# 512 more columns of the down product as seven products of 256, one up group less, and two weight sums made in DRAM

## The chip, the core and the metric

The kernel runs on one core of a Trainium2 chip. The metric is device time in microseconds (us) of one execution, the median over several runs. PE is TensorE, PEld its weight loads, DVE is VectorE, ACT is ScalarE, POOL is GpSimd, and SP is SyncE, whose queue sends out nearly all DMAs.

## What is computed

One encoder block over 272 positions (16 meta tokens and 256 others), width 2048, in float32: a normalisation, two kinds of attention side by side, an output projection with residual, and then a gated MLP with residual. The change lies in the MLP, which in the reference is

```python
def conv_glu(x, w_gate, w_up, conv_w, conv_b, w_down):
    L = x.shape[1]
    g = x @ w_gate
    u = x @ w_up
    pad = CONV_W // 2
    gp = jnp.pad(g, ((0, 0), (pad, pad), (0, 0)))
    gc = conv_b
    for i in range(CONV_W):
        gc = gc + conv_w[i] * gp[:, i:i + L]
    return (jax.nn.silu(gc) * u) @ w_down
...
    h = h + conv_glu(rmsnorm(h, ffn_norm_g[l]), w_gate[l], w_up[l], conv_w[l], conv_b[l], w_down[l])
return h[:, N_META:]
```

`w_gate` and `w_up` are 2048 x 5632, `w_down` is 5632 x 2048, and the 256 positions that are not meta tokens are returned.

## The kernel before

**Precision.** A float32 product is made of single-pass products: each operand is split into a high part (rounded, ScalarE) and a low part (the rest, VectorE), and high x high, high x low and low x high are summed in PSUM. Weights are therefore loaded in pieces of up to 1024 columns of 128 rows (512 KB; `raw`), split by ScalarE into `whi` (L239, called by `split_hi`) and by VectorE into `wlo` (L243, `split_lo`), and used by PE. There are four `whi` and four `wlo` buffers, so the splits run at most four pieces ahead of PE, and six `raw` buffers in the MLP.

**Plain tiles.** Gate tiles (128 of the 5632 columns) take three matmuls of 258 columns for each 128 rows of weights (L607 to L609). Plain up and down tiles take two (`mm2`, L1875 and L1876): the high weights against the high and low activations side by side, 512 columns, then the low weights against the high activations, 256. The last down tile takes three of 256. I call each such set of matmuls for one 128 x 128 weight tile a block. A piece of 1024 is eight blocks.

**Seven products.** Where a 2 x 2 block product would need eight products, a scheme makes it of seven, from sums of blocks on both sides. Here a pair of contraction tiles (256 rows) against Q columns is cut into 2 x 2 blocks: the weights' quarters are Q/2 wide, the activations' quarters are 128 positions. Four sums of weight quarters are made by VectorE (`weight_sums`), four sums of activation quarters in `value_sums`; those are kept as split parts in DRAM (`s_up`, `s_down`) or in the unfilled end of the activation buffer (`near`), and loaded back into two buffers (`sin`). A pair is a `RowPair`, its pieces are `Quarters`, and `scheme_products` issues 7 x 3 matmuls (L279). The kernel before uses it in two places:

- *Up groups* (`QUADS`): six groups of four up tiles (512 columns), each 8 pairs; products of 256 columns. The two pieces of a pair hold 768 and 1024 columns: the three quarters used as they are, and the four sums. The sums take VectorE one operation of 512 and two of 256 for each pair.
- *The wide group*: 1024 of the 2048 down columns (`SF`), 22 pairs; products of 512 columns. A pair has pieces of 1024, 512, 1024 and 1024 columns, and its sums take one operation of 1024 and two of 512.

Weights' quarters lie in the order A, B, C, D = upper left, upper right, lower right, lower left; the sums are C or B less A or B, and further differences of these.

**Order.** A list `work` holds all MLP pieces in PE's order. First come gate and up tiles, plain, up to the first group. Then a stretch for each group: its 16 pieces are spread evenly among the gate and up pieces of the stretch (six tiles for the first four groups, eight for the last two). Then the down product: three plain pieces (`AHEAD`), the 88 pieces of the wide group among plain down pieces, and eight plain pieces at the end (`BEHIND`). A plain down tile has 44 blocks: five pieces of 1024 and one of 512. The instruction order of every engine is written out by a planner in the kernel (`Flow`), from its own costs; on the chip each engine runs its list in that order and waits by semaphores. One list `pieces` orders the loads, too (`load_weights`, L489 on SP's queue).

**Buffers.** When the last up tile has been used, the memory of the split activations of the MLP's input becomes two buffers of 2048 columns for the wide group's weights (`quarters`) and two for their sums (`sums4`). Of the eight PSUM banks, an up group holds four until its output is taken, the wide group seven.

**Outputs.** Plain down tiles come out transposed (`down_out`): for all but the last one, ScalarE copies and three POOL additions and products scale them and add the residual, then a DMA writes them. The wide group's output (`scheme_out`) is combined by VectorE from the seven banks, scaled by ScalarE, added to the residual by POOL and written by four DMAs. `EARLY` pairs of the MLP input's activation sums go to DRAM before the attention's buffers are free; the residual of the wide columns is transposed beforehand.

Of the kernel before, what the change touches and what calls it, by code (L numbers as in the profile page):

```python
# [45 lines left out]
SF = 1024  # L46
ST = SF // P
QUADS = (4,10,16,22,28,36)


def near_to(g):

    return sum(f <= FC - KC + 2 * g for f in (*QUADS, FC)[1:])

# [3 lines left out]
AHEAD, BEHIND = 3, 8  # L58
PAIR_PRIO = 3
# [147 lines left out]
def encoder_block(ctx: ExitStack, tc: tile.TileContext, io):  # L207
# [138 lines left out]
    class Quarters(Piece):  # L346
# [3 lines left out]
        def __init__(self, pair, products, *segments):  # L350
            self.pair, self.products, self.segments = pair, products, segments
            self.slices([n for _, _, n in segments])
            self.n = sum(n for _, _, n in segments)
            self.there = [
                pair.loaded if kind == "raw" else pair.summed[a + n > 2 * pair.q]
                for kind, a, n in segments
            ]

        def release(self):
            self.pair.used(self.segments[0][0])  # L360

        def views(self, i):
            kind, a, n = self.segments[i]
            t = self.parts[i]
            src = self.pair.raw if kind == "raw" else self.pair.sums
            return src[:, a : a + n], self.hi[:, t], self.lo and self.lo[:, t]

    class RowPair:


        def __init__(self, src, g, q):
            self.src, self.g, self.q = src, g, q
            self.loaded, self.summed, self.ev_S = Event(), [Event(), Event()], Event()
            if q == PW // 2:
                self.pieces = [
                    Quarters(self, (3, 2), ("raw", 2 * q, 2 * q)),
                    Quarters(self, (1,), ("raw", 0, q)),
                    Quarters(self, (5, 7), ("sums", 0, 2 * q)),
                    Quarters(self, (6, 4), ("sums", 2 * q, 2 * q)),
                ]  # L380
                self.slots = {"raw": quarters, "sums": sums4}
            else:
# [4 lines left out]
                self.slots = {"raw": raws, "sums": raws}  # L387
            n = len(self.pieces) // 2
            self.left = {"raw": n + 1, "sums": n}

        def used(self, kind):
            self.left[kind] -= 1
            if self.left[kind] == 0:
                fl.put(self.slots[kind], getattr(self, kind))

    quarters, sums4, s_parts = Slots([]), Slots([]), Slots([])
# [45 lines left out]
    for w, f in enumerate(QUADS):  # L442

        g, end = f // 2, (*QUADS, FC)[w + 1] // 2
# [4 lines left out]
        for i in range(KC // 2):  # L449
            r = RowPair(io["w_up_s"][w][i], i, PW // 4)  # L450
            r.first, r.last, r.of, r.quad = i == 0, i == KC // 2 - 1, "up", f
# [3 lines left out]
        lead, tail = 3, 4 if w == len(QUADS) - 1 else 2  # L455
# [12 lines left out]
    scheme = []  # L468
    for g in range(FC // 2):
        r = RowPair(io["w_down_s"][g], g, PW // 2)  # L470
        r.first, r.last, r.of, r.near = g == 0, g == FC // 2 - 1, "down", False
        scheme += [(p, "scheme", r, 0) for p in r.pieces]
    n = len(others) - BEHIND
    work += others[:AHEAD]
    for i in range(AHEAD, n):
        k = 4 if others[i - 1][2] != others[i][2] else 2
        work += scheme[:k] + [others[i]]
        del scheme[:k]
    work += scheme + others[n:]
# [25 lines left out]
    def load_pair(r):  # L505
        if r.of == "up":
            r.raw, r.sums = yield raws, 2
        else:
            r.raw = yield from one(quarters)
        def load_S():  # L510
            if r.near:
                r.ev_S = ev_near[r.g]
                return
            r.S = yield from one(s_parts)
            src, saved = saved_sums[r.of][r.g]
# [4 lines left out]
        if r.of == "up":  # L520
            yield from load_S()
        for a in range(0, 4 * r.q, PW):
            yield "sp", 600
            ev = r.loaded if a + PW == 4 * r.q else Event()
            load(r.raw[:, a : a + PW], r.src[:, a : a + PW], ev, nc.sync)
        if r.of == "down":
            yield from load_S()
        fl.spawn(weight_sums(r), (lambda: 0) if r.of == "up" else 2)

    def weight_sums(r):  # L530
        yield r.loaded
        if r.of == "down":
# [1682 lines left out]
```

## Time and profile before

| | us |
|---|---|
| median of three runs (1109.08 to 1109.53) | 1109.18 |
| the profiled execution | 1109.0 |
| its span, from its first to its last instruction | 1107.1 |

The granted TensorE clock is 1.0 throughout. The page's slices show DMA and its rate over the span, 27.7 us each:

```profile
DMA  9553434443654696656645667677588697777862
GB/s 327 194 172 124 147 128 151 139 162 134 230 189 159 205 338 212 216 188 207 255 167 184 236 209 277 211 272 244 181 300 298 225 331 254 250 263 263 280 251 76
```

The first row is the mean busy share of the 16 DMA engines in tenths (9 is 90% or more), the second what they moved. The attention lies in slices 1 to about 11, the output projection behind it, the MLP from about 400 us (slice 15) on, and the wide down group from about 870 us to 1083 us. Rows of a window are: the window, its length, then for each engine busy time and number of instructions, the granted clock, the DMA share and GB/s. A timeline row has start, duration, engine, line, operation, what it writes and reads, the count, and in brackets the engine's idle time before it. A duration may reach into the next instruction's start, so that the time that one instruction adds is read from start to start.

### The profile page before, as it was taken

To read this page: it belongs to the slowest core of one execution; us is meant where nothing else is said; L and a number is where in the kernel's file an instruction comes from. 1 tells how busy PE (TensorE), PEld (TensorE's weight loads), DVE (VectorE), ACT (ScalarE), POOL (GpSimd) and SP (SyncE) were. 2 spreads that over 40 slices of the span, in tenths; PEclk is the share of its full clock that TensorE was granted. 3 is DMA by queue.
4 is the path that set the end of the run, shared out by engine and by line. 5 is a ranking of instruction groups with operands and counts; after the bars stand their busy time and mean duration, and the time that the engine had idled before them with its cause. 6 is when DMAs were issued, how large, how long until landed. Compare 5 with 4: busy or idle time off the path is not lost.

```text
span 1107.1 us, 21940 instructions
## 1 busy us (share of the span) xinstructions
PE 1099.9 (99%) x8094; PEld 1046.2 (95%) x8094; DVE 1000.8 (90%) x1857; ACT 740.7 (67%) x1490; POOL 140.9 (13%) x202
## 2 busy tenths in 40 slices
PE   9999999999999999999999999999999999999998
PEld 9999999999999999999999999999999888888888
DVE  8979888888878989999999999988999999999984
ACT  8788979798647676656665665666556565655663
POOL 3211222121433400000000000000000011100114
PEclk9999999999999999999999999999999999999999
DMA  9553434443654696656645667677588697777862
GB/s 327 194 172 124 147 128 151 139 162 134 230 189 159 205 338 212 216 188 207 255 167 184 236 209 277 211 272 244 181 300 298 225 331 254 250 263 263 280 251 76
DMA packets 72372, 239.36 MB, mean 216 GB/s; under 512 B 8137, under 2 KB 12745, under 8 KB 72265
## 3 DMA queue, kind: packets, MB, share of 16 engines
q1 hardware_dynamic: 71976, 237.69, 61.8%
q8 instruction: 63, 1.03, 0.4%
q14 instruction: 45, 0.36, 0.1%
q10 hardware_dynamic: 288, 0.27, 0.1%
HBM read 219.44 MB, written 17.83 MB: 214 GB/s over the span
## 4 chain that ended last, share of the span: by engine, by line
PE 81%; DVE 9%; ACT 5%; DMA 3%; issue 2%; POOL 0%; DVEq 0%; SPq 0%; ACTq 0%; POOLq 0%
PE bank L279 21%; PE bank L607 13%; PE bank L609 13%; PE bank L608 13%; PE bank L1875 12%; PE bank L1876 6%; DVE wlo L243 4%; PE bank L285 2%; ACT whi L239 2%; DMA s_down<-sums 1%; ACT scr L239 1%; DVE mt L243 1%; DVE scr L251 1%; DMA s_up<-sums 1%; DVE raw L243 1%
## 5 line engine op out<-in xcount | busy, mean ns | idle before, releaser
L239 ACT ACTIVATE whi<-raw 128x512 fp32r<-128x512 f32 (+2 forms) x479 | 357.9, 764 | 148.5 <-PE bank L608 58.5
L243 DVE TENSOR_TENSOR wlo<-raw,whi 128x512 fp32r<-128x512 f32 (+2 forms) x479 | 413.9, 884 | 34.3 <-ACT whi L239 33.1
L607 PE MATMUL bank<-hl,whi 128*128 128x258 f32 (+1 forms) x1208 | 347.9, 288 | 0.1
L609 PE MATMUL bank<-hl,wlo 128*128 128x258 f32 (+1 forms) x1208 | 343.4, 284 | 1.1 <-DVE wlo L243 1.0
L608 PE MATMUL bank<-hl,whi 128*128 128x258 f32 (+1 forms) x1208 | 343.7, 285 | 0.0
L609 PEld LDWEIGHTS bank<-hl,wlo 128*128 128x128 f32 x1208 | 229.7, 190 | 2.2 <-DVE wlo L243 1.9
L608 PEld LDWEIGHTS bank<-hl,whi 128*128 128x128 f32 x1208 | 229.3, 190 | 0.1
L607 PEld LDWEIGHTS bank<-hl,whi 128*128 128x128 f32 x1208 | 228.3, 189 | 0.8 <-ACT scr L239 0.3
L239 ACT ACTIVATE whi<-quarters 128x1024 fp32r<-128x1024 f32 x88 | 81.5, 951 | 64.3 <-PE bank L1875 46.2
L1875 PE MATMUL bank<-hl,whi 128*128 128x512 f32 x320 | 113.6, 395 | 0.0
L279 PE MATMUL bank<-whi,act 128*128 128x256 f32 (+1 forms) x420 | 111.4, 317 | 0.0
L1875 PE MATMUL bank<-act,whi 128*128 128x512 f32 x308 | 109.9, 397 | 0.0
L243 DVE TENSOR_TENSOR wlo<-quarters,whi 128x1024 fp32r<-128x1024 f32 x88 | 99.4, 1154 | 9.6 <-ACT whi L239 9.2
L267 POOL TENSOR_TENSOR mt<-mt,mt 128x256 f32<-128x256 f32 x7 | 7.7, 1095 | 651.0 <-ACT mt L239 651.0
L1876 PE MATMUL bank<-hl,wlo 128*128 128x256 f32 x320 | 89.7, 280 | 0.0
L1876 PE MATMUL bank<-act,wlo 128*128 128x256 f32 x308 | 86.5, 281 | 0.0
L279 PE MATMUL bank<-whi,sin 128*128 128x512 f32 (+1 forms) x272 | 83.4, 355 | 0.0
L279 PEld LDWEIGHTS bank<-whi,act 128*128 128x128 f32 x420 | 74.1, 188 | 6.0
L1875 PEld LDWEIGHTS bank<-hl,whi 128*128 128x128 f32 x320 | 60.1, 188 | 12.8
L1875 PEld LDWEIGHTS bank<-act,whi 128*128 128x128 f32 x308 | 57.8, 188 | 13.8
L279 PE MATMUL bank<-whi,hl 128*128 128x256 f32 x288 | 66.5, 280 | 0.0
L279 PE MATMUL bank<-wlo,act 128*128 128x256 f32 (+1 forms) x210 | 66.2, 315 | 0.0
(282 smaller groups left out, 2176.0 us busy)
## 6 DMA issues: line engine op xcount, KB each, us to landing
raw<-in_w_gate SPq DMA_DIRECT2D x83, 512.0 KB, 5.3
raw<-in_w_in SPq DMA_DIRECT2D x52, 512.0 KB, 3.7
raw<-in_w_up_s SPq DMA_DIRECT2D x44, 512.0 KB, 4.7
quarters<-in_w_down_s SPq DMA_DIRECT2D x44, 512.0 KB, 7.0
raw<-in_w_up SPq DMA_DIRECT2D x34, 512.0 KB, 5.9
raw<-in_w_out SPq DMA_DIRECT2D x32, 512.0 KB, 3.7
raw<-in_w_down SPq DMA_DIRECT2D x32, 512.0 KB, 5.6
s_down<-sums SPq DMA_DIRECT2D x22, 512.0 KB, 5.1
```

Of the source, the lines that this page charges most:

```text
L239: nc.scalar.activation(out, in_, f, **kw)
L243: nc.vector.tensor_tensor(out, a, b, op)
L251: nc.vector.scalar_tensor_tensor(out, a, s, b, op0, op1)
L267: nc.gpsimd.tensor_tensor(out, a, b, op)
L279: nc.tensor.matmul(o, l, r, start=start, stop=stop)
L285: nc.tensor.transpose(o, i, ident[:n, :n])
L607: nc.tensor.matmul(ps, whi, xhi, start=start, stop=False)
L608: nc.tensor.matmul(ps, whi, xlo, start=False, stop=False)
L609: nc.tensor.matmul(ps, wlo, xhi, start=False, stop=stop)
L1875: nc.tensor.matmul(ps, whi, x, start=start, stop=False)
L1876: nc.tensor.matmul(ps[:, :n], wlo, x[:, 0, :], start=False, stop=stop)
```

## The change

- The scheme's down columns are 1536 (`SF`), not 1024: the wide group keeps 1024 (`SL`), and 512 more (`SM`) are made by 22 pairs with products of 256 (`mid`), as an up group is. Four plain down tiles go (eight become four).
- There are five up groups, not six (`QUADS`, the last one over tiles 28 to 31), so four more up tiles are plain. Each of the five stretches has six tiles. From tile 34 (`MID`) the gate and up tiles are all plain, and the new pairs' 44 pieces lie among them: four pieces of the rest first (`MID_LEAD`), then 38 among the other 36, the last six among five plain down pieces; two more plain pieces follow before the wide group (`AHEAD` 7, `MID_GAP` 2).
- The wide group's 88 pieces are spread among 13 plain pieces, the last of which stands behind them, and four plain pieces end the list (`BEHIND` 4).
- All signs in the scheme are turned so that sums are additions. For the wide group the first two sums (the 1024 columns of A + B and B + C) are made in DRAM during the attention: SP copies A and B of each pair to `early`, DRAM to DRAM, and POOL sends a DMA that adds B and C to it, 22 of each, the second waiting for the first; each load of a wide pair then brings lower half (1024), the first quarter alone (512) and `early` (1024). VectorE makes the other two sums (two operations of 512).
- The freed memory becomes eight `raw` buffers of 1024 columns, so that all 14 serve every kind of piece; a load of activation sums no longer stands in front of its pair's weights; the activation sums of the last pair are taken from SBUF by the new products, and their buffer is then a third one for such loads. The last five pairs' activation sums have a higher priority in the planner.
- An output buffer is reserved when a group's last pair begins; `EARLY` is 6, and 12 quarter tiles of the residual are transposed beforehand, not 8. The new columns' output (`mid_out`) is combined by VectorE as an up group's, scaled by ScalarE, added to the residual by POOL in four operations, and written by two DMAs.

```diff
-SF = 1024
+SF = 1536
 ST = SF // P
-QUADS = (4,10,16,22,28,36)
+SL = 1024
+SM = SF - SL
+QUADS = (4, 10, 16, 22, 28)
+MID = 34
...
-AHEAD, BEHIND = 3, 8
-PAIR_PRIO = 3
+AHEAD, BEHIND = 7, 4
+MID_LEAD, MID_LEFT, MID_GAP = 4, 6, 2
+LAST = FC // 2 - 1
...
+    rest = []
+    for g in range(MID // 2, FC // 2):
+        rest += tile_pair("gate", g) + tile_pair("up", g)
+    mid = down_pairs("mid", io["w_down_m"], PW // 4)
+    scheme = down_pairs("down", io["w_down_s"], PW // 2)
+    work += rest[:MID_LEAD]
+    work += spread(mid[: len(mid) - MID_LEFT], rest[MID_LEAD:])
+    work += spread(mid[len(mid) - MID_LEFT :], others[: AHEAD - MID_GAP])
+    work += others[AHEAD - MID_GAP : AHEAD]
     n = len(others) - BEHIND
...
+    work += spread(scheme, others[AHEAD:n])
+    work += others[n:]
...
+        if r.wide:
+            r.at["lower"] = yield from one(raws)
             yield "sp", 600
+            load(r.at["lower"], r.src[:, 2 * q :], r.loaded, nc.sync)
+            r.at["upper"] = yield from one(raws)
+            n = q if r.early else 2 * q
+            yield "sp", 600
+            load(r.at["upper"][:, :n], r.src[:, :n], r.first_loaded, nc.sync)
+            fl.spawn(load_S())
+            r.at["two"], r.at["more"] = yield raws, 2
+            if r.early:
+                src, done = early_sums[r.g]
+                yield done
+                yield "sp", 600
+                load(r.at["two"], src, r.summed[0], nc.sync)
...
+            yield from TT(m[:, :q], low[:, :q], t[:, :q], ALU.add)
+            yield from TT(m[:, q:], m[:, :q], low[:, q:], ALU.add)
...
-        yield from TT(t[:, : 2 * q], raw[:, q : 3 * q], raw[:, : 2 * q], ALU.subtract)
+        t, raw = r.at["sums"], r.at["raw"]
+        yield from TT(t[:, : 2 * q], raw[:, q : 3 * q], raw[:, : 2 * q], ALU.add)
...
-        fl.put(quarters if i < 2 else sums4, t)
+        for a in (0, PW):
+            fl.put(raws, t[:, a : a + PW])
...
+    def sums_in_dram():
+        copied = [Event() for _ in early_sums]
+        for g in range(FC // 2 + 2):
+            if g < FC // 2:
+                yield "sp", 600
+                load(early_sums[g][0], io["w_down_s"][g][:, :PW], copied[g], nc.sync)
+            if g >= 2:
+                t, done = early_sums[g - 2]
+                yield copied[g - 2]
+                yield "pool", 1000
+                src = io["w_down_s"][g - 2][:, PW // 2 : 3 * PW // 2]
+                nc.gpsimd.dma_start(t, src, accum_op=ALU.add)
+                fl.set(done, 8000.0)
+            fl.cur.t += 12000.0
...
-            fl.spawn(pair_sums(f // 2), PAIR_PRIO)
+            fl.spawn(pair_sums(f // 2), 3 if f // 2 < LAST - 4 else 0)
...
-    EARLY = 4
+    EARLY = ST // 2
...
+    def mid_out(P7, b):
+        out = yield from reserved()
+        U = quarters_of(out)
+        yield from seven(P7, b, U)
+        for i in range(2):
+            for j in range(2):
+                yield from ACT(U[i][j], U[i][j], AF.Copy, scale=s_2t[:, i : i + 1])
+                yield from PTT(U[i][j], U[i][j], res[SL // (2 * P) + j][:, i, :], ALU.add)
+            yield "sp", 600
+            nc.sync.dma_start(io["out"][i][:, SL:], out[:, i * SM : (i + 1) * SM])
```

More of the change, by code (lines that the diff above doesn't have):

```diff
@@ L1951, in scheme_products @@
                     yield ev
-            start = r.first and (r.of == "down" or n in (3, 1, 7, 4))
-            stop = r.last and (r.of == "down" or n in (2, 5, 6, 4))
+            start = r.first and (r.wide or n in (3, 1, 7, 4))
+            stop = r.last and (r.wide or n in (2, 5, 6, 4))
             yield from MM(product3(sums7[n], a, (p.hi[:, t], p.lo[:, t]), start, stop))
```

202 lines of the change are left out of this document (125 added, 77 removed).

## The prediction

> **What bounds the kernel now.** I read the page first: busy times, then the chain.
>
> ```profile
> span 1107.1 us, 21940 instructions
> PE 1099.9 (99%) x8094; PEld 1046.2 (95%) x8094; DVE 1000.8 (90%) x1857; ACT 740.7 (67%) x1490; POOL 140.9 (13%) x202
> ...
> PE 81%; DVE 9%; ACT 5%; DMA 3%; issue 2%; POOL 0%; DVEq 0%; SPq 0%; ACTq 0%; POOLq 0%
> ...
> raw<-in_w_in SPq DMA_DIRECT2D x52, 512.0 KB, 3.7
> ...
> quarters<-in_w_down_s SPq DMA_DIRECT2D x44, 512.0 KB, 7.0
> ```
>
> PE is busy 99% of the span, but the page warns that a busy PE need not be at its peak. So I looked at the stages by windows (PE, PEld, DVE, ACT, POOL busy with counts, granted clock, DMA share, GB/s) and at who waits for whom after 400 us.
>
> ```profile
> 40.00:350.00 310.00, 309.17 (x2550) 305.65 (x2549) 264.16 (x664) 244.96 (x716) 70.98 (x125) 1.00 0.47 158
> ...
> 575.00:645.00 70.00, 69.23 (x548) 67.49 (x547) 67.55 (x125) 43.29 (x70) 0.00 (x0) 1.00 0.59 205
> 645.00:712.00 67.00, 66.91 (x530) 65.19 (x529) 65.31 (x124) 40.75 (x67) 0.00 (x0) 1.00 0.64 226
> 712.00:805.00 93.00, 93.00 (x720) 90.19 (x719) 84.86 (x155) 55.63 (x90) 0.00 (x0) 1.00 0.71 244
> ...
> 895.00:1083.00 188.00, 187.97 (x934) 157.54 (x934) 175.01 (x177) 110.43 (x129) 24.24 (x18) 1.00 0.76 266
> ```
>
> ```profile
> ACT whi L239 <- PE bank L1875: 72.7, 52, 3.1
> ...
> PE bank L609 <- DVE wlo L243: 0.8, 1, 0.8
> ```
>
> Apart from an idle POOL, the longest wait in the MLP is ScalarE's for PE to give a split weight buffer back; the one wait listed for PE's matmuls is 0.8 us. The weights are there before PE wants them, so matmul columns set the time. But a six-tile up group (645 to 712) has VectorE 65.31/67 = 97% busy: there is little room beside PE. An eight-tile group (712 to 805) leaves 9%, the wide down stage 7%.
>
> **The change part by part.** *Products.* PE's pace comes from short stretches of one kind: three windows (the first counts line 279 on PE alone, the second line 1875 alone, the third everything), and two rows of a timeline between which twelve 512-column products start.
>
> ```profile
> 500.00:502.47 2.47, 2.47 (x21) 1.00 0.56 187
> ```
> ```profile
> 1082.97:1087.18 4.21, 4.21 (x12) 2.07 (x11) 1.00 0.23 90
> ```
> ```profile
> 1087.19:1103.30 16.11, 16.00 (x134) 15.79 (x132) 6.67 (x10) 6.22 (x13) 11.16 (x11) 1.00 0.20 74
> ```
> ```profile
> 1080.19 0.39 PE L279 MATMUL bank<-whi,sin 128*128 128x512 f32 x1
> ...
> 1082.96 0.39 PE L1875 MATMUL bank<-act,whi 128*128 128x512 f32 x1
> ```
>
> A 256-column product takes 2.48/21 = 0.118 us, a plain up or down block (512 columns, then 256) 4.22/12 = 0.352 us, a block of the last down tile (three times 256) 16.0/44 = 0.36 us, a 512-column product 2.77/12 = 0.231 us. The order of the two programs gives the counts. Up: one group less is 8 x 21 = 168 products of 256 less, and 4 tiles x 16 = 64 plain blocks more: -19.9 + 22.5 = +2.6 us. Down: 4 x 44 = 176 plain blocks less, 22 x 21 = 462 products of 256 more: -62.0 + 54.7 = -7.3 us. The 462 wide products stay; 8 transposes go with the group and 8 come with two more residual tiles. PE's work: **-4.7 us**, spread over the down half.
>
> *VectorE.* Its pitch is the start-to-start time, since an instruction's end overlaps the next start:
>
> ```profile
> 501.32 1.02 DVE L243 TENSOR_TENSOR wlo<-raw,whi 128x512 fp32r<-128x512 f32 x2
> 502.25 0.42 DVE L243 TENSOR_TENSOR sums<-mt,sums 128x256 fp32r<-128x256 f32 x1
> 502.59 0.28 DVE L243 TENSOR_TENSOR mt<-mt,mt 128x128 f32<-128x128 f32 x1
> ...
> 503.12 1.22 DVE L243 TENSOR_TENSOR wlo<-raw,whi 128x1024 fp32r<-128x1024 f32 x1
> 504.25 0.69 DVE L243 TENSOR_TENSOR more_raw<-raw 128x512 f32<-128x512 f32 x1
> 504.97 0.42 DVE L243 TENSOR_TENSOR more_raw<-raw,more_raw 128x256 f32<-128x256 f32 x1
> 505.43 0.42 DVE L243 TENSOR_TENSOR more_raw<-more_raw,raw 128x256 f32<-128x256 f32 x1
> 505.77 1.22 DVE L243 TENSOR_TENSOR wlo<-raw,whi 128x1024 fp32r<-128x1024 f32 x1
> ```
>
> So 1.13 us for 1024, 0.72 for a 512 sum with its successor waiting on it, 0.46 and 0.34 for the 256 sums; 501.32 to 502.25 holds a 512 and a 256 split, which with 0.34 for the 256 (502.25 to 502.59) leaves 0.59. The order: splits +2 of 1024, +10 of 512, +14 of 256 = +12.9 us; sums -22 of 1024 (the part now made in DRAM), +14 of 512, +28 of 256 (half at each pitch) = -24.9 + 10.1 + 11.2 = -3.6 us; four more 256 gating products +1.4. In all about **+11 us** on 1000.8, on an engine that must finish nearly 5 us earlier. By stage, VectorE against PE:
> - Six-tile groups: five instead of four, each as 645 to 712 shows (97%).
> - Tiles 34 to 43 with the new products among them: 19 pairs x 3.6 (splits 2.06, sums 1.52) + 4 gate pairs x 6.8 (four splits, six small operations of 0.34 to 0.4) + 5 up pairs x 8.5 (the same and their own activation sums, 1.9) = 138 us; PE 19 x 21 x 0.118 + 4 x 96 x 0.121 + 5 x 32 x 0.352 = 150 us: 92%.
> - Wide stage: a pair's splits 4.0 and remaining sums 1.3 give 22 x 5.3 = 117, twelve plain pieces 12.5, the 512 columns' output 2.4: 132 us; PE 462 x 0.231 + 88 blocks = 138 us: 95%.
>
> All stay under the 97% that a group already carries with PE 99.9% busy. One thing eases the last stage: POOL slows VectorE.
>
> ```profile
> 960.68 0.81 POOL L267 TENSOR_TENSOR mt<-mt,mt 128x256 f32<-128x256 f32 x1 [27.21 <-ACT mt L239]
> ...
> 962.71 1.61 POOL L267 TENSOR_TENSOR mt<-mt,res 128x256 f32<-128x256 f32 x1
> ```
> ```profile
> 962.03 1.69 DVE L243 TENSOR_TENSOR wlo<-raw,whi 128x1024 fp32r<-128x1024 f32 x1
> 963.64 1.75 DVE L243 TENSOR_TENSOR wlo<-quarters,whi 128x1024 fp32r<-128x1024 f32 x1
> ...
> 966.46 1.21 DVE L243 TENSOR_TENSOR wlo<-quarters,whi 128x1024 fp32r<-128x1024 f32 x1
> ```
>
> Beside POOL's three operations per plain down tile, two splits take 0.5 us more each; four such tiles go, four POOL additions come.
>
> *DMA.* A wide pair loads 1.31 MB and its 0.52 MB of activation sums; with 12 plain pieces that is 22 x 1.83 + 6 = 46 MB in 138 us, 333 GB/s, against 266 GB/s now. The same memory now serves 14 single buffers, and before the wide stage come seven plain pieces (20 us of PE) that need little, so I estimate 5 MB fetched ahead: 41/138 = 297 GB/s is needed. What DMA gives when pushed:
>
> ```profile
> 390.00:400.00 10.00, 9.75 (x57) 8.43 (x56) 8.73 (x18) 7.78 (x13) 0.00 (x0) 1.00 0.98 359
> 400.00:410.00 10.00, 10.00 (x80) 9.75 (x79) 8.94 (x22) 8.11 (x17) 0.00 (x0) 1.00 1.02 403
> ```
>
> So it fits, at some 85% share. Landing gets later than 7.0 us; 14 buffers, four to a pair, are over three pairs (over 15 us of PE). I take 0.3 us, bounds 0 and 3.
>
> *Sums in DRAM.* During attention, 22 copies (DRAM to DRAM, on SP) and 22 accumulating DMAs (on POOL, each waiting for its copy, sent out two steps earlier) are added, which the trace does not show. Nearest: the page's loads and the share (158 GB/s at 0.47, so 0.52 MB is 1.5 us of all 16 engines). Counted once per DMA they add 66 us to 310 x 0.47 = 146; counted per read and per write, five times 0.52 MB, 165 us: a share of 0.68 to 1.0. Behind SP's copies stand weight loads, which land in 3.7 us and have five buffers of some 3 us of PE work each; behind POOL's DMAs stand the attention's small sums, and POOL is idle 239 of 310 us. PE cost 0 to 2 us; I take 0.2, nearer the low end, as the loads may be late by several us unseen. By the fit in the Trainium skill (DMA: Bandwidth & Descriptors, Anatomy of one DMA) a DMA from POOL takes 2.0 us + bytes/436e3, an estimated 3.2 us for 0.52 MB; by it the sum stays as it is.
>
> *Waits.* The last pair's activation sums come straight from SBUF, but their second half stands in VectorE's order behind the split two pieces ahead of the product that reads it. That split waits for PE to free its buffer, and ScalarE's and VectorE's 1.0 + 1.1 + 0.3 us must fit in the plain piece between (8 x 0.352 = 2.8 us): 0 to 0.7 us once, I take 0.3. The fifth full group: 0.3 (the four now lose about 1 us, above all 575 to 645), bound 1.2.
>
> *Tail.* Five plain pieces (36 blocks, 13 us), not eight, follow the last wide product.
>
> ```profile
> 1087.39 3.49 POOL L267 TENSOR_TENSOR quarters<-quarters,resT 128x256 f32<-128x256 f32 x2 [24.01 <-ACT quarters L239]
> ...
> 1095.12 3.51 POOL L267 TENSOR_TENSOR quarters<-quarters,resT 128x256 f32<-128x256 f32 x5
> ```
>
> Now the wide output ends on POOL at 1098.6, 15.7 us after the last wide product (1082.96), with 3 operations of another tile between and splits ahead of its additions. Without those it ends some 11 to 13 us after, as PE does, while the plain tile's own end comes 4 us later (PE ends near 1103.2 of 1107.1). Cost 0; 2 if POOL is not done.
>
> **Sum.** 1109.0 (the profiled execution: 1107.1 plus 1.9 around it) - 4.7 + 0.3 + 0.2 + 0.3 + 0.3 = 1105.4; the median 1109.18 lies 0.2 higher: **1105.6 us**. With no added stall, and the 0.8 us at 575 to 645 gone, 1103.6; with every upper bound (3 + 2 + 0.7 + 1.2 + 2), 1113.
>
> **The rivals.**
> - *VectorE becomes the bound.* For: 97% groups are more, the 95% stage follows. Against: PE idles 0.09 us in 645 to 712 at that load. If 3% more of VectorE's 132 and 138 us came than I count, the wide stage would be at 98% and lose perhaps 3 to 4 us in bursts: about 1109.
> - *DMA becomes the bound in the wide stage, slower.* It decides below 297 GB/s; the gain is gone at 41/142.7 = 287. At the 266 GB/s that the stage moves now: 41/266 = 154, 16 us over PE's 138: 1121. For: 266 came at 0.76, so full share is 350. Against: 359 and 403 above.
> - *The DRAM sums hold up the attention.* If a copy with its accumulation delayed PE by 0.15 us on average, +3.3: 1108.7. For: a share near 1.0 at the upper count. Against: buffers and POOL's idle time.
> - *Weight loads pace PE, slower.* The change has 70 matmuls more (8094 now), each with its load. Were PE paced by loads, 1107/8094 = 0.137 us each: +9.6, 1118.6. Against: 0.118 us for 256 columns and 0.231 for 512 follow the columns. This is the rule of the Trainium skill (Perfetto Trace Analysis, Identifying the Most-Contended Engine): judge TensorE by LDWEIGHTS busy, here 95%, not by matmul busy. The pace by width disagrees with a bound on loads.
>
> **How the numbers follow.** Forecast 0.60, VectorE 0.14, DRAM sums 0.08, DMA 0.12 (half of it under 1113), weight loads 0.03, and 0.03 that stalls eat the gain elsewhere. Measurement tells 0.2% (2.2 us) from no change: faster is under 1107.0, the forecast and some of VectorE's and DRAM's milder ends: 0.65; same 0.17; slower 0.18, DMA, loads and the worse ends. Range 1103.6 to 1111, which leaves out the full DMA and load cases.
>
> **What would show it.** Right: L1875's act blocks 308 to 132, hl 320 to 384; PE busy near 1095, at 99% in every stage after 400; VectorE busy 1005 to 1015; DMA share 0.8 to 0.9 in the last 150 us; the end 4 us after the last matmul. Wrong: PE idle before a wide product with a DMA as releaser, ScalarE waiting for loads before 350, or VectorE at 99% with PE waiting for splits.

## The result, and the profile after

| | before | after |
|---|---|---|
| median, us | 1109.08 (1108.18 to 1109.53, 5 runs) | 1120.09 (1119.88 to 1125.11, 5 runs) |
| the profiled execution, us | 1109.0 | 1123.05 |
| its span, us | 1107.1 | 1121.2 |

The change made the kernel slower: the ratio of the mean times is 1.0114, 95% interval 1.0091 to 1.0137. The forecast of 1105.6 us and its range were wrong. In the changed kernel the helper lines have moved: VectorE's is L247, ScalarE's L243, the scheme's matmuls are L283 and SP's loads L514. The page of after, by its busy times, its chain and its loads:

```profile
span 1121.2 us, 22349 instructions
PE 1102.6 (98%) x8164; PEld 1048.7 (94%) x8164; DVE 1008.2 (90%) x1907; ACT 755.9 (67%) x1518; POOL 142.8 (13%) x216
...
PE 73%; DVE 11%; DMA 9%; ACT 3%; issue 2%; SPq 1%; POOL 0%; DVEq 0%; ACTq 0%; POOLq 0%
...
raw<-in_w_in SPq DMA_DIRECT2D x52, 512.0 KB, 4.8
```

The chain that ended last is PE for 73% of the span, not 81%, and DMA for 9%, not 3%. A PE that waits can't be read from a busy share of 98%, so I took the trace's list of matmuls: for each pair of neighbours the time from start to start, less what that shape takes undisturbed (0.230 us for 512 columns, 0.121 for 258, 0.118 for 256, and so on for the others). The sum of the undisturbed times is 1090.6 us before and 1086.4 after. What lies above it I call PE's excess, by stage of the kernel:

| PE's excess, us | to 70 us | 70 to 250 | 250 to the first group | groups, to the first wide product | wide stage to the end | sum |
|---|---|---|---|---|---|---|
| before | 3.6 | 3.3 | 0.6 | 1.6 | 2.2 | 11.2 |
| after | 2.5 | 10.8 | 5.3 | 3.2 | 7.7 | 29.5 |

PE's work fell by 4.2 us and its waits rose by 18.3, together 14.1, as the spans say. The waits came in two places. The first is the attention. Two rows of the windows view, 60 to 300 us and 960 to 1080 us, before and then after (length, busy times with counts, clock, DMA share, GB/s):

```profile
60.00:300.00 240.00, 239.17 (x1973) 235.88 (x1973) 211.04 (x556) 204.74 (x635) 54.73 (x107) 1.00 0.45 151
960.00:1080.00 120.00, 120.00 (x598) 100.80 (x597) 111.83 (x111) 70.90 (x83) 15.63 (x12) 1.00 0.75 263
```
```profile
60.00:300.00 240.00, 234.21 (x1914) 230.26 (x1913) 206.61 (x547) 202.02 (x627) 62.69 (x120) 0.99 0.75 213
960.00:1080.00 120.00, 117.03 (x536) 94.17 (x535) 109.46 (x118) 78.30 (x89) 11.61 (x9) 1.00 0.90 318
```

The DMA view of the stretch 60 to 300 us, again before and then after, shows who suffers: `scr<-scr`, 32 KB each, by which the attention exchanges the halves of its rotary embedding (RoPE) between partitions. Such a transfer landed in 2.3 us and now takes 5.5 (medians). The row of q0 has packets, MB and the share of the 16 engines that the accumulating DMAs held.

```profile
scr<-scr SPq DMA_DIRECT2D x16, 32.2 KB, 2.3
```
```profile
q0 software_dynamic: 2304, 8.39, 21.7%
...
early<-in_w_down_s SPq DMA_DIRECT2D x16, 512.0 KB, 6.1
early<-in_w_down_s POOLq DMA_DIRECT2D x16, 512.0 KB, 7.7
scr<-scr SPq DMA_DIRECT2D x16, 32.2 KB, 5.5
```

The timeline of after around 75 us, VectorE and then PE, shows what a late exchange costs:

```profile
69.97 1.37 DVE L247 TENSOR_TENSOR wlo<-raw,whi 128x512 fp32r<-128x512 f32 x2
74.73 0.43 DVE L247 TENSOR_TENSOR scr<-scr,consts 128x258 f32<-128x258 f32 x1 [3.38 <-DMA scr<-scr]
75.07 0.69 DVE L247 TENSOR_TENSOR wlo<-raw,whi 128x512 fp32r<-128x512 f32 x1
75.68 0.70 DVE L259 CAST sq8r<-sq 128x8 fp32r<-128x8 f32 x1
```
```profile
73.32 0.28 PE L663 MATMUL bank<-hl,wlo 128*128 128x272 f32 x1
76.43 0.17 PE L283 MATMUL bank<-ones_r,sq8r 128*4 128x2 f32 x1 [2.82 <-DVE sq8r L259]
```

VectorE stands for 3.38 us at an operation whose exchange has not landed. Behind it in VectorE's list is a small cast that PE wants, so PE stands for 2.82 us, though neither the cast nor the matmul reads the exchange. The second place is the wide stage, in the timeline of after:

```profile
1017.24 2.91 DVE L247 TENSOR_TENSOR wlo<-halves,whi 128x512 fp32r<-128x512 f32 x2
1021.65 0.69 DVE L247 TENSOR_TENSOR halves<-raw,halves 128x512 f32<-128x512 f32 x1 [1.51 <-DMA halves<-early]
1022.26 2.35 DVE L247 TENSOR_TENSOR wlo<-halves,whi 128x1024 fp32r<-128x1024 f32 x2
```
```profile
1023.53 0.50 PE L283 MATMUL bank<-wlo,sin 128*128 128x512 f32 x1 [1.33 <-DVE wlo L247]
```
```profile
1012.91 0.37 SPq L514 DMA_DIRECT2D halves<-early  x1
```

Here the operation at the head is a sum of weights that reads the half made in DRAM, and the split behind it is what PE waits for. Matched in order of issue, the load of `early` went out at 1012.91 and its sum ran at 1021.65. Over the 22 pairs this distance has a median of 7.1 us, for a transfer that takes 6.8 (960 to 1080 us). SP did not hold the loads back of itself: from 950 to 1090 us its queue stood for 83.9 us until a split of VectorE's gave a buffer back.

```profile
halves<-early SPq DMA_DIRECT2D x12, 512.0 KB, 6.8
```
```profile
SPq L514 <- DVE wlo L247: 83.9, 66, 4.9
```

In the kernel before, the second load of a pair's quarters went out a median of 9.7 us ahead of the pair's first sum, and such loads landed in 7.0.

Both kernels' lists are written by the same planner with the same belief about transfers (in `load`; times in ns):

```python
        t = max(dma_free[0], fl.cur.t) + nc_bytes / 350.0
        dma_free[0] = t
        queue.dma_start(out, src)
        fl.set(ev, t + 2000.0 - fl.cur.t)
```

By it an exchange lands after 2.1 us and 512 KB after 3.5. Before, that was about right in the attention (2.3 and 3.7). After, it is too short there by a factor of 1.4 for the weights (4.8) and of 2.6 for the exchanges (5.5).

### The profile page after: what moved, and what is told of

Its sections match the earlier page's. It is cut to its first block, busy times and chain, and to the rows that moved or that the text cites. A ratio compares the mean times of both kernels' runs of the same rounds, so it can differ in the third digit from the quotient of the medians.

```text
span 1121.2 us, 22349 instructions
## 1 busy us (share of the span) xinstructions
PE 1102.6 (98%) x8164; PEld 1048.7 (94%) x8164; DVE 1008.2 (90%) x1907; ACT 755.9 (67%) x1518; POOL 142.8 (13%) x216
## 4 chain that ended last, share of the span: by engine, by line
PE 73%; DVE 11%; DMA 9%; ACT 3%; issue 2%; SPq 1%; POOL 0%; DVEq 0%; ACTq 0%; POOLq 0%
PE bank L283 17%; PE bank L661 14%; PE bank L662 14%; PE bank L663 14%; PE bank L1955 8%; DVE wlo L247 7%; PE bank L1956 4%; PE bank L289 2%; DMA raw<-in_w_down_m 1%; DMA halves<-early 1%; DMA raw<-early 1%; ACT whi L243 1%; DMA scr<-scr 1%; DMA more_raw<-early 1%; DVE raw L247 1%
## 5 line engine op out<-in xcount | busy, mean ns | idle before, releaser
L243 ACT ACTIVATE whi<-raw 128x512 fp32r<-128x512 f32 (+2 forms) x511 | 381.1, 765 | 138.8 <-PE bank L662 49.2
L247 DVE TENSOR_TENSOR wlo<-raw,whi 128x512 fp32r<-128x512 f32 (+2 forms) x511 | 444.7, 891 | 26.5 <-ACT whi L243 25.4
L663 PEld LDWEIGHTS bank<-hl,wlo 128*128 128x128 f32 x1208 | 230.4, 191 | 0.9 <-DVE wlo L247 0.8
L283 PE MATMUL bank<-whi,act 128*128 128x256 f32 (+1 forms) x560 | 144.4, 308 | 0.0
L283 PEld LDWEIGHTS bank<-whi,act 128*128 128x128 f32 x560 | 98.9, 189 | 5.9
L243 ACT ACTIVATE whi<-halves 128x1024 fp32r<-128x1024 f32 (+2 forms) x68 | 63.5, 944 | 37.7 <-PE bank L283 22.4
L283 PE MATMUL bank<-wlo,act 128*128 128x256 f32 (+1 forms) x280 | 86.2, 308 | 0.0
L283 PE MATMUL bank<-whi,sin 128*128 128x256 f32 (+1 forms) x312 | 85.0, 326 | 0.1
L247 DVE TENSOR_TENSOR wlo<-halves,whi 128x1024 fp32r<-128x1024 f32 (+2 forms) x68 | 75.0, 1124 | 1.0 <-ACT whi L243 0.6
L1956 PEld LDWEIGHTS bank<-hl,wlo 128*128 128x128 f32 x384 | 73.2, 191 | 0.9 <-DVE wlo L247 0.9
L243 ACT ACTIVATE whi<-more_raw 128x1024 fp32r<-128x1024 f32 (+2 forms) x60 | 51.6, 868 | 23.1 <-PE bank L283 6.4
L247 DVE TENSOR_TENSOR wlo<-more_raw,whi 128x1024 fp32r<-128x1024 f32 (+2 forms) x60 | 58.5, 987 | 3.2 <-ACT whi L243 3.2
L283 PEld LDWEIGHTS bank<-whi,sin 128*128 128x128 f32 x312 | 55.3, 188 | 6.1 <-issue 0.3
```

The costliest lines, as they stand in the source:

```text
L243: nc.scalar.activation(out, in_, f, **kw)
L247: nc.vector.tensor_tensor(out, a, b, op)
L283: nc.tensor.matmul(o, l, r, start=start, stop=stop)
L663: nc.tensor.matmul(ps, wlo, xhi, start=False, stop=stop)
L1956: nc.tensor.matmul(ps[:, :n], wlo, x[:, 0, :], start=False, stop=stop)
```

## The experiments

Each is the changed kernel with one edit, or with an earlier experiment's edit and one more. The kernel before ran beside them, with medians from 1107.98 to 1108.62 us. Ratios are to it, with their 95% intervals. A kernel called complete makes the whole output.

**e1_no_sums_made.** The 44 DMAs are left out, while the planner still gives them their places; the wide pairs load unsummed quarters of the same size, so the output is not the reference's.

```diff
-        queue.dma_start(out, src)
+        if queue is not None:
+            queue.dma_start(out, src)
...
-                load(r.at["two"], src, r.summed[0], nc.sync)
+                load(r.at["two"], r.src[:, :PW], r.summed[0], nc.sync)
...
-                load(early_sums[g][0], io["w_down_s"][g][:, :PW], copied[g], nc.sync)
+                load(early_sums[g][0], io["w_down_s"][g][:, :PW], copied[g], None)
...
-                nc.gpsimd.dma_start(t, src, accum_op=ALU.add)
```

> Leaves out the 22 copies and the 22 accumulating DMAs during the attention; the wide pairs load the two quarters themselves in place of their sums (same size), so 1024 output columns are not the product. Everything else stands in the same order. Theory A (the 44 DMAs make the attention's small exchanges land late, and PE waits for what hangs on them): scr<-scr lands in some 2.5 us again, not 5.5; the first product of the first up group starts at 434 to 438 us (445.8 in the changed kernel, 433.7 before); total 1109 to 1113, with the wide stage as it is (its excess of about 7 us stays). Rival B (the planner's other order, POOL's place or the two more residual tiles cost it): the first group stays near 445 and the total near 1120.

1117.42 us, ratio 1.0076 (1.0061 to 1.0091). The exchanges landed in 2.9 us again and the first group began 6.7 us sooner than in after, nearly as the theory said. The time did not follow (1109 to 1113 were expected): without the 44 DMAs much of the loss remains. The wide stage kept its excess (8.4 us).

**e2_copies_alone.** Only the additions are left out (the last line of the diff above); the wide pairs load an unsummed half.

> Makes the 22 copies on SP's queue but leaves out POOL's 22 accumulating DMAs (the 1024 wide columns are not the product). Theory A1 (the copies stand in front of the small exchanges in SP's rings): keeps most of the delay, first group at 441 to 446, total 1116 to 1120. Rival A2 (the accumulating DMAs take the engines): nearly all of it goes, first group at 434 to 438, total 1109 to 1113.

1117.12 us, 1.0081 (1.0056 to 1.0105). The copies alone add 0.6 us of excess to e1's in the stretch 70 to 250 us. So of the 5.4 us that e1 takes away there, 4.8 go with the additions alone, as rival A2 said. That the time lies in A1's range does not speak for A1: A2's range left out what e1 still loses elsewhere.

**e3_copies_act_queue.** Complete; the copies go out on ScalarE's queue and no longer stand in SP's.

```diff
-                load(early_sums[g][0], io["w_down_s"][g][:, :PW], copied[g], nc.sync)
+                load(early_sums[g][0], io["w_down_s"][g][:, :PW], copied[g], nc.scalar)
```

> The same kernel, complete, with the 22 copies sent out on ScalarE's queue and not SP's; all else in the same order. Theory A1 (order in SP's rings): scr<-scr lands in about 3 us, first group near 437, total 1111 to 1114. Rival A2 (the engines' time is shared whatever the queue): first group stays at 443 to 446, total 1118 to 1121.

1123.08 us, 1.0135 (1.012 to 1.015). The exchanges landed in 6.2 us, no sooner, so it isn't the copies' place in SP's queue that makes them late. From 60 to 300 us:

```profile
scr<-scr SPq DMA_DIRECT2D x16, 32.2 KB, 6.2
```

The excess is 11.2 us between 70 and 250 us; in the wide stage it is 10.0, which no run explains.

**e4_sums_later.** Complete; the 44 DMAs go out during the up groups, every 16 us.

```diff
-            fl.cur.t += 12000.0
+            fl.cur.t += 16000.0
...
-        yield pieces[18].loaded
-        fl.spawn(sums_in_dram())
...
         fl.set(ev_mlp)
+        fl.spawn(sums_in_dram())
```

> The same kernel, complete, with the 44 DMAs sent out from the start of the MLP on, one pair each 16 us (about 400 to 790 us), not during the attention. Theory A: the attention is as before (first group at 434 to 438), the up groups carry a DMA share of 0.85 to 0.95 where nothing small is waited for, the wide stage stays as it is: total 1109 to 1113. Rival (any 58 MB more at a busy time cost the same): PE waits for weights in the groups instead, total 1116 to 1122.

1145.55 us, 1.0328 (1.0309 to 1.0348), far above both ranges. The attention was as before (excess 3.4 us between 70 and 250), the groups lost 30.9.

**e5_not_planned** and **e6_two_not_loaded.** In both the 44 DMAs are left out and the planner does not know of them either; as in e1, the output is not the reference's. In e6 (second diff, against e5) the load of the two sums is left out from the seventh wide pair on, too.

```diff
-        yield pieces[18].loaded
-        fl.spawn(sums_in_dram())
...
-                src, done = early_sums[r.g]
-                yield done
                 yield "sp", 600
-                load(r.at["two"], src, r.summed[0], nc.sync)
+                load(r.at["two"], r.src[:, :PW], r.summed[0], nc.sync)
```
```diff
-                yield "sp", 600
-                load(r.at["two"], r.src[:, :PW], r.summed[0], nc.sync)
+                if r.g < 6:
+                    yield "sp", 600
+                    load(r.at["two"], r.src[:, :PW], r.summed[0], nc.sync)
+                else:
+                    fl.set(r.summed[0])
```

> Leaves out the 44 DMAs that make the sums in DRAM, and this time the planner does not know of them either (in e1_no_sums_made it still gave them their places on SyncE and GpSimd); the wide pairs load the same number of bytes, unsummed quarters, so the output is not the reference's. Theory 'order': part of what e1 still lost in the attention (PE stood 0.63 us at 111.4, 0.92 and 0.63 us at 123) came from the order that the planner wrote around the 44 DMAs; without it the PE excess between 100 and 150 us falls from 3.07 to about 1, and the time is 1115 to 1116. Rival 'no order effect': 1117 to 1118, with the stalls at 111 and 123 still there. Both expect the wide stage to keep its 7 to 8 us of excess.

> As e5_not_planned, but from the seventh wide pair on the 512 KB of the two sums are not loaded (the products and VectorE read whatever stands in the buffer; the output is not the reference's). VectorE's and TensorE's work stays the same; the wide stage's traffic falls by about 0.5 of 1.79 MB a pair. Theory 'DMA': the waits of the wide stage are for transfers that land late at 318 GB/s and a share of 0.9; without a quarter of the traffic the PE excess between 950 and 1100 us falls from about 8 to at most 2.5 us and the time is 5 to 7 us below e5_not_planned, 1109 to 1111. Rival 'VectorE full': VectorE is busy for 91 to 95% of that stage and its order alone makes PE wait; the excess stays at 6 to 8 us and the time within 1.5 us of e5_not_planned.

e5: 1115.19 us, 1.0065 (1.0049 to 1.0081). The stalls at 111 and 123 us are gone: 2 of e1's 5.4 us between 70 and 250 came from the order alone. e6: 1115.64 us, 1.006 (1.004 to 1.0079), no faster. The theory that the wide stage waits for the rate of the transfers fell, and the numbers of its rival, a full VectorE, came out. Its window, and VectorE's waits from 950 to 1090 us, in e6:

```profile
960.00:1080.00 120.00, 116.00 (x531) 93.42 (x529) 110.77 (x120) 77.42 (x87) 6.31 (x6) 1.00 0.77 262
```
```profile
DVE halves L247 <- DMA halves<-in_w_down_s: 2.7, 4, 1.4
DVE halves L247 <- DMA raw<-in_w_down_s: 2.6, 2, 2.2
```

At 262 GB/s and a share of 0.77, about what the kernel before had, VectorE still waited 5.3 us for loads, and PE's excess in the wide stage was 8.1 us. So VectorE was not simply full: it stood idle at sums whose loads had not landed.

**e7_landing_5us.** Complete; the planner takes 5.0 us, not 2.0, for a landing after 40 us of its time.

```diff
-        fl.set(ev, t + 2000.0 - fl.cur.t)
+        fl.set(ev, t + (2000.0 if t < 40000.0 else 5000.0) - fl.cur.t)
```

> Complete. One number of the planner is changed: from 40 us on it takes a transfer to land 5.0 us after its bytes, not 2.0, so that it puts instructions that need the data later in the queues of VectorE and ScalarE. Theory 'blocked queues': the waits are made where an instruction that needs a transfer stands at the head of VectorE's or ScalarE's queue before its data is there, and work that is ready stands behind it; with later places the time falls by 5 to 10 us, to 1110 to 1115. Rival 'late is late': the transfers themselves pace the stage, and another order moves the waits but does not remove them: 1118 to 1123.

1115.87 us, 1.0071 (1.0054 to 1.0088) against the changed kernel's 1.0114: a gain, just short of what the theory asked for. Excess: 7.9 between 70 and 250 us, 1.7 until the first group, 6.3 in the groups, 4.1 in the wide stage.

**e8_sums_on_vector.** Complete; no sums in DRAM, VectorE makes all four.

```diff
-            self.wide, self.early = q == PW // 2, of == "down"
+            self.wide, self.early = q == PW // 2, False
...
-        yield pieces[18].loaded
-        fl.spawn(sums_in_dram())
```

> Complete. The part 'two of the wide group's sums of weights in DRAM' is undone: no early DMAs, each wide pair loads its four quarters and VectorE makes all four sums (44 more 128x512 sums, about 0.61 us each, 27 us). Theory: the attention gets back its 7 to 9 us, but the wide stage of 142 us, in which VectorE stood idle for about 12 us, becomes VectorE's and is 12 to 18 us longer: 1123 to 1130. Rival 'DMA bound wide stage': the stage waits for transfers, VectorE's idle time hides most of the 27 us, and the traffic per pair falls by 0.25 MB: 1113 to 1118.

1124.76 us, 1.0152 (1.0137 to 1.0167), as the theory said: excess 3.3 in the attention, 19.1 in the wide stage. There VectorE is busy for 119.05 of 120 us:

```profile
960.00:1080.00 120.00, 111.62 (x504) 89.37 (x503) 119.05 (x140) 70.41 (x80) 7.91 (x5) 0.99 0.80 267
```

**e9_pool_plain_copies.** All DMAs go out as in the changed kernel, but POOL's only copy; the addition is left out.

```diff
-                nc.gpsimd.dma_start(t, src, accum_op=ALU.add)
+                nc.gpsimd.dma_start(t, src)
```

> As the changed kernel, with its order, its issues and its queues, but GpSimd's 22 DMAs only copy: the addition into DRAM is left out, so that the wide pairs load half of the sum (the output is not the reference's). Theory 'bytes of the accumulation': an accumulating DMA held 21.7% of the DMA engines between 60 and 300 us for 8.39 MB, a copy of the same bytes on ScalarE's queue 10.9%; with plain copies the RoPE exchanges land in 4 us or less and not 5.5, the PE excess between 70 and 250 us falls from 10.8 to 6 to 8, and the time is 1115 to 1118. Rival 'GpSimd's queue': it is the issuing on GpSimd or its software queue that holds the attention up: the excess stays at 10 to 11 and the time at 1119 to 1122.

1117.47 us, 1.0088 (1.007 to 1.0106): the theory of the accumulation's bytes, except that the exchanges took 5.0 us and not 4. Queue q0 of e9 from 60 to 300 us:

```profile
q0 software_dynamic: 2304, 8.39, 11.9%
```

The same packets and bytes as in the changed kernel held 11.9% of the engines, not 21.7%.

**e10_later_two_sums_buffers** and **e11_later_two_buffers_5us.** Complete. As e4, but one of the 14 weight buffers becomes a second buffer for activation sums on their way to DRAM; e11 has e7's edit, too.

```diff
-        for t in tiles(mpool, 1, [P, PW], "more_raw"):
-            fl.put(raws, t)
+        for t in tiles(mpool, 1, [P, PW], "more_sums"):
+            fl.put(combined, t)
```

> Complete. As e4_sums_later (the 44 DMAs during the groups), but one of the 14 weight buffers of the MLP becomes a second buffer for the sums of the values that go to DRAM. Theory 'one buffer': the 27 us that e4 lost in the groups came from ScalarE standing at the single sums buffer until its store had landed (34 us of waits, up to 6.7 each), with VectorE behind it; with two buffers at least 18 of these are gone: 1115 to 1126. Rival 'weights late': the groups wait because at a DMA share of 0.8 to 0.9 their weights come late, and a buffer less makes that worse: 1138 to 1150.

> Complete. As e10_later_two_sums_buffers, and the planner takes 5.0 us for a landing as in e7_landing_5us. Theory 'blocked queues': the attention is rid of the DRAM sums (3.4 us of PE excess between 70 and 250), the stores of the sums no longer hold ScalarE up (1.7 until the first group), the wide stage has the 4 us of e7; with 3 to 8 us in the groups that makes 1107 to 1113, the best of the versions so far. Rival: the groups, where VectorE is busy for 97%, cannot do with late weights whatever the order is: 1116 to 1135.

1150.98 us, 1.0389 (1.0373 to 1.0404), and 1164.33 us, 1.0518 (1.0489 to 1.0546). Both theories fell. In e10 ScalarE's 34 us at the sums buffer are gone, and the groups lose 32 us all the same. The window 450 to 800 us of e5, without the DMAs, and of e4, and e10's waits from 440 to 810 us:

```profile
450.00:800.00 350.00, 348.45 (x2726) 338.80 (x2726) 336.18 (x617) 216.70 (x345) 0.00 (x0) 1.00 0.66 220
```
```profile
450.00:800.00 350.00, 331.72 (x2552) 319.62 (x2551) 314.44 (x574) 199.35 (x319) 13.93 (x17) 0.99 0.82 256
```
```profile
ACT whi L243 <- DMA raw<-in_w_gate: 26.9, 15, 4.1
ACT whi L243 <- DMA raw<-in_w_up_s: 25.2, 15, 4.3
...
DVE raw L247 <- DMA raw<-in_w_up_s: 15.4, 12, 3.3
```

The groups live on six weight buffers (five in e10), and VectorE has 4% to spare. With 0.16 more DMA share e10's weights land too late. How much of that is the buffer that it gave away was not separated, so whether e4's own loss came from the sums buffer, where ScalarE's longest waits stand, or from late weights is not shown.

**e12_5us_not_in_groups** and **e13_half_the_sums.** Complete. e12 is e7 with 2.0 us kept in the groups. e13 is e12 with every second pair's sums made by VectorE, and the DMAs for the others 24 us apart.

```diff
-        fl.set(ev, t + 2000.0 - fl.cur.t)
+        short = t < 40000.0 or 430000.0 < t < 860000.0
+        fl.set(ev, t + (2000.0 if short else 5000.0) - fl.cur.t)
```
```diff
-            self.wide, self.early = q == PW // 2, of == "down"
+            self.wide, self.early = q == PW // 2, of == "down" and g % 2 == 0
...
-        for g in range(FC // 2 + 2):
+        for g in range(0, FC // 2 + 4, 2):
...
-            fl.cur.t += 12000.0
+            fl.cur.t += 24000.0
```

> Complete. As e7_landing_5us, but between 430 and 860 us of its own time the planner keeps to 2.0 us, since e7 gained in the attention and the wide stage and lost about 3 us of PE time in the groups. Theory 'blocked queues, each stage by itself': the groups go back to 3 us of excess, the attention keeps e7's 8 and 2, the wide stage its 4: 1111.5 to 1114. Rival 'the wide stage gained only because its loads were ordered from earlier on': its excess goes back to 7 or 8 us and the time to 1115 to 1119.

> Complete. As e12_5us_not_in_groups, but only every second wide pair has its two sums made in DRAM (11 copies and 11 additions, 24 us apart); VectorE makes the others in the wide stage (22 more 128x512 sums, 13.5 us). Theory 'share of the DMA engines': the attention loses half as much, its excess between 70 and 250 us falls from 8 to about 5.5, and VectorE's 12 idle us of the wide stage take most of the 13.5: 1110 to 1114. Rival 'VectorE': the wide stage has no idle time that it can give, and gets 6 us or more longer: 1115 to 1120.

e12: 1113.67 us, 1.0057 (1.0035 to 1.0079), inside its theory's range and the best complete version with this change; 0.0057 of the ratio, 6.3 us, are gone. e13: 1118.19 us, 1.0086 (1.0066 to 1.0106), as its rival said: VectorE was busy for 49.93 of the 50 us from 1000 on. In e12's wide stage, by its window, its loads and VectorE's waits from 950 to 1090 us, where this one row is left:

```profile
960.00:1080.00 120.00, 119.40 (x553) 97.75 (x551) 113.81 (x123) 79.56 (x92) 9.13 (x8) 1.00 0.94 334
```
```profile
halves<-early SPq DMA_DIRECT2D x9, 512.0 KB, 6.6
```
```profile
DVE wlo L247 <- ACT whi L243: 7.8, 16, 1.3
```

More bytes per second than in the changed kernel, a landing as late (6.6 us against 6.8), and no wait of VectorE for a load. The transfers did not get faster; the sums stand later in VectorE's list, a median of 10.8 us after their load's issue and not 7.1, with splits that are ready in front of them.

All stages side by side, each row from one profiled execution; that of after and that of e9 lie 3 us above their medians (for the exchange, the median landing from 60 to 300 us; for the share, that of the same stretch):

| | share | exchange, us | excess 70 to 250 | 250 to first group | groups | wide stage |
|---|---|---|---|---|---|---|
| before | 0.45 | 2.3 | 3.3 | 0.6 | 1.6 | 2.2 |
| e5, no sums | 0.47 | 2.3 | 3.4 | 3.2 | 4.3 | 7.8 |
| e1, only their places | 0.47 | 2.9 | 5.4 | 3.0 | 3.8 | 8.4 |
| e2, copies | 0.58 | 3.7 | 6.0 | 2.6 | 3.6 | 7.6 |
| e9, copies twice | 0.69 | 5.0 | 7.5 | 6.1 | 3.8 | 7.1 |
| after | 0.75 | 5.5 | 10.8 | 5.3 | 3.2 | 7.7 |
| e7 | 0.77 | 5.0 | 7.9 | 1.7 | 6.3 | 4.1 |
| e12 | 0.77 | 4.7 | 7.0 | 1.7 | 4.5 | 4.2 |
| e13, half the sums | 0.62 | 4.2 | 7.3 | 2.4 | 5.3 | 7.2 |

How far such a stage repeats can be read from five profiles whose attention has none of the 44 DMAs, nor places for them (before, e4, e5, e6, e8): between 70 and 250 us they lie within 3.3 and 3.5 us.

The wide stage can be sorted by the plan. In the three kernels that are planned with 5.0 us there and make both sums in DRAM it has 4.1 or 4.2 us (e7, e11, e12), though e11 has 13 weight buffers and not 14. Planned with 2.0 us, it has 7.1 to 10.0 with 14 buffers (e1 to e6, e9 and after), and 14.7 with 13 (e10). e8 and e13, in which VectorE makes more of the sums, stand apart with 19.1 and 7.2.

## Why the prediction was wrong

**Right.** *Products:* -4.7 forecast, -4.2 in the trace. *VectorE:* 1008.2 us busy, forecast 1005 to 1015, and the 97% groups cost nothing: from the first product of the first group to that of the fifth it is 268.3 us before and 267.7 after. That the two sums could not stay on VectorE is shown by e8. *Waits:* the new products' last pair runs at 951 us, and PE's excess from 900 us to the first wide product is 0.4 us in all, so the wait at its sums lies within its bounds; so does the fifth group, with some 0.6 us. *Tail:* 0; the end is 4.1 us after the last matmul, 3.9 before. *Weight loads as the bound:* no; in the 514 us from the first group to the wide stage the undisturbed times by width leave 3.2 us of excess. (Some of the prediction's sums are off by 0.1: the up and down parts are +2.7 and -7.4, with the same -4.7 in all, and the time without any added stall is 1103.7.)

**The step "behind SP's copies stand weight loads ... behind POOL's DMAs stand the attention's small sums", which gave 0.2 us with 2 as the upper bound, failed.** The weight loads did come later (3.7 to 4.8 us) and PE did not feel it, as was said. But I asked only what has buffers. The exchanges have none: each is issued when its data is made, and the plan has its reader 2.1 us later. In the rows of the table from e5 to after, landing and excess go up together, and from e1 on the share with them. It cost 10.8 - 3.4 = 7.4 us between 70 and 250 and 2.1 more until the first group; 2 of the 7.4 are the order that the planner wrote around the 44 DMAs (e1 less e5). By place, after has some 4 us more than e5 between 70 and 90 us, which is the wait shown above and the slower clock behind it; 2.5 around 120 us, where e1 has the same stalls without the transfers; and 1.6 around 190 us, of which e1 has 0.7. The profiled execution of after is 3 us above its median; by the ratios the DRAM sums cost 1.0114 - 1.0065, some 5.4 us, which the two intervals leave uncertain by 3. The trace of before had the rows for this: `scr<-scr` with 2.3 us, and the share of 0.68 to 1.0 that I had worked out myself. The rival that named this place had a price of 3.3 us, too low, and a chance of 0.08. POOL's DMAs landed in 7.7 us (5.7 as plain copies, e9), not in the estimated 3.2.

The Trainium skill (DMA: Bandwidth & Descriptors, Anatomy of one DMA) splits a DMA that GpSimd issues into a fixed part of about 2.0 us and bytes/436e3, so an estimated 2.1 us for 32 KB. The exchanges go out on SP's queue, for which the fit was not made; their landing is near it at a share of 0.45 (2.3 us) and not at 0.75 (5.5).

**The step "14 buffers, four to a pair, are over three pairs (over 15 us of PE)", behind the 0.3 us of the wide stage, failed, too.** The rate was forecast well (297 GB/s at 85%; measured 318 at 0.90), and so was what spoke against the DMA rival: the stage is not bound by the rate (e6). But the number of buffers does not say how far ahead a load goes out, for a buffer is taken until VectorE has split what is in it, and one of a pair's four is taken with the load of `early` and stays empty until the sums are made. The trace does say it: 7.1 us, about one pair, and a landing of 6.8 uses that up. The cost is 7.7 - 2.2 = 5.5 us. e12 gives back 3.5 of it by order alone, and e11 shows the same with a buffer less; that VectorE is then busy for 113.81 of 120 us may hold the rest, but that was not separated.

**A term was missing.** `EARLY` at 6 sends two more sets of activation sums through the single `sums` buffer, and ScalarE's list stands at it until the store has landed. From 345 to 440 us, in before, after and e12:

```profile
ACT sums L239 <- DMA s_up<-sums: 7.8, 3, 3.0
```
```profile
ACT sums L243 <- DMA s_up<-sums: 11.3, 4, 4.0
```
```profile
ACT sums L243 <- DMA s_up<-sums: 1.6, 1, 1.6
```

e5, without any DRAM sums, loses 2.6 us here against before (3.2 and 0.6); with the planner's 5.0 us the loss falls to 1.1. In after, PE's waits of 2.2 and 1.2 us that end at 399.4 and 400.7 follow in the chain on such a store, which landed at 394.6. But the kernel before waited for its stores, too, and lost 0.6 us. That the two more sets are the cause is therefore not shown: a kernel with 4 there and the rest of the change was not tried.

**Could the change pay?** PE's work is 4.2 us less, so the excess of all stages would have to stay under 11.2 + 4.2 = 15.4 us. The lowest excess of each stage in any complete kernel that makes its sums in DRAM during the attention is 2.5, 7.0, 1.7, 2.5 (e3) and 4.1 us, 17.8 in all. No version here beats the kernel before.

## What to carry to other kernels

Before adding traffic beside a busy stage, list its transfers by how long before their use they are issued: here those without a buffer ahead of them, 32 KB each, lost, and not the weight loads. Where an order is written out from planned times, an operation placed at the planned landing of a transfer blocks all work behind it in its engine's list when the transfer is late; placing it later gave back 3.5 us in the wide stage, and cost 3 us in the groups, where VectorE has no idle time for it (e7). The number of buffers is not the distance of the loads; read the distance from the issue rows, and from what the issuing queue waits for.

## What the runs showed of the hardware

- An accumulating DMA, DRAM to DRAM, held the 16 engines for about twice as long as a copy of the same 8.39 MB: 21.7% against 11.9% of 240 us (after and e9).
- A short wait of PE can cost more than itself. After the wait of 3 us at 76 us, and after waits of 2.2 and 1.2 us that ended at 399.4 and 400.7, the granted clock fell for some microseconds; windows of after:

```profile
78.00:80.00 2.00, 2.00 (x10) 2.00 (x10) 2.00 (x8) 1.61 (x6) 0.00 (x0) 0.50 0.74 234
80.00:84.00 4.00, 4.00 (x31) 4.00 (x30) 3.12 (x9) 3.85 (x10) 1.15 (x3) 0.89 0.05 12
```
```profile
402.00:406.00 4.00, 4.00 (x17) 3.43 (x15) 2.83 (x6) 2.72 (x6) 0.00 (x0) 0.61 0.62 220
406.00:410.00 4.00, 4.00 (x27) 3.60 (x26) 2.79 (x6) 2.42 (x6) 0.00 (x0) 1.00 0.81 211
```

From 402 to 406 PE issued 17 matmuls, in the next 4 us 27. Shorter waits in after did not do this: after those of 0.9 and 0.6 us at 126 us, and of 1.5 us at 1023 us, the clock of the next microseconds is 1.00.
